# Attention heads: the key and query loads of a head as two transfers of 64 rows each, in place of one with an outermost count of two

## The chip, the cores and the metric

The kernel runs on one core of one Trainium2 chip. The metric is the device time of one execution in microseconds (us), smaller is better. Matrix products run on TensorE (PE in the profile; PEld is its weight load), element-wise work on VectorE (DVE), ScalarE (ACT) and GpSimd (POOL). Transfers between DRAM and the on-chip buffer are issued from the queues of SyncE (SP) and of GpSimd, and 16 DMA engines carry them out.

## The reference

One layer of a decoder trunk: a norm, a combined input projection, four token mixers (two attentions, a recurrent branch, attention into a memory), gates, and a gated MLP. The change touches the loads of the two attentions with 16 heads of 64 columns over 1024 tokens:

```python
        fq = _rms(_heads(proj("fox_q"), FOX_HEADS), fox_q_norm_g[l]).astype(f32)
        fk = _rms(_heads(proj("fox_k"), FOX_HEADS), fox_k_norm_g[l]).astype(f32)
...
        # _fox_attention, per block of 128 queries
        logits = jnp.einsum('bhqd,bhkd->bhqk', qi, k) * scale + (fi[..., :, None] - cum_f[..., None, :])
        logits = jnp.where(k_pos[None, :] <= q_pos[:, None], logits, -jnp.inf)
        p = jax.nn.softmax(logits, axis=-1)
        return jnp.einsum('bhqk,bhkd->bhqd', p, v)
...
        # _stick_breaking_attention, per block of 128 queries
        z = jnp.einsum('bhqd,bhkd->bhqk', qi, k) * scale
        log_1m_beta = jnp.where(causal, jax.nn.log_sigmoid(-z), 0.0)
        excl = lax.cumsum(log_1m_beta, axis=3, reverse=True) - log_1m_beta
        weights = jnp.where(causal, jnp.exp(jax.nn.log_sigmoid(z) + excl), 0.0)
        return jnp.einsum('bhqk,bhkd->bhqd', weights, v)
```

## The kernel before

Values are kept as a rounded part and a remainder (two numbers per value), and products are made from two or three matmuls. The kernel works in stages: projections that need a norm of their own (from 0 to about 450 us), the recurrent branch (to about 750 us), the attention stage (about 750 to 1895 us), then the branch projections and the MLP.

In the attention stage three lists of groups run one after the other: the memory attention (`Mem`, 750 to 870 us), the 16 fox heads and the 16 stick-breaking heads (`Head`). Each head has four groups of two query blocks. A group makes scores (`score`: matmuls `S<-kx,qq` on L182, two per piece of up to 512 keys), a softmax or a scan on ACT, DVE and POOL, transposes of the weights (`turn`, `T` on L848, evacuated on L613 and L614) and the product with the values (`value`, `PV` on L182). Between these, matmuls of the remaining projections and gates (`mm<-hTh,wh` and the like, also L182) are put in as filler, one by one, by `fill`. The order of all PE work of the stage is written out when the program is made, by a planner in `build` that keeps a model of the engines' times (`clock`, `spend`); on the chip it is fixed, and PE takes its instructions in that order.

The loads of a head are all issued from the POOL queue: `load_q` loads the queries `qq` (L736, 1 MB: 64 rows of 8 KB, twice, into the two halves of the 128 partitions) and for fox the row of forget sums `fb`, copied to 128 partitions (L733); `load_k` loads `kx` (L750, 512 KB: the rounded keys into partitions 0 to 63, the remainders into 64 to 127); `load_v` loads `vx` (L756, 512 KB, 128 partitions as the outermost count). In `load_q` and `load_k` the source has an outermost count of two, and under it 64 rows. `qq`, `kx` and `vx` have two buffers each. A head's loads are issued when the head two before it has finished its last scores (`qq`, `kx`) or its last values (`vx`).

POOL also computes. For a fox head it makes `fd` from `fb` (`offsets`, L744) ahead of the head's scores; this is issued when the head before it is halfway through its scores. For a stick-breaking head it makes the two triangular masks of every query block (`affine_select`, L829), for which the scan on DVE (L831) waits. POOL takes its loads and its computing in one order, so a `fd` that waits for `fb` holds back the loads behind it.

Of the kernel before, what the change touches and what calls it, by code (L numbers as in the profile page):

```python
# [7 lines left out]
F32 = mybir.dt.float32  # L8
# [8 lines left out]
S = 1024  # L17
# [4 lines left out]
HD = 64  # L22
# [40 lines left out]
def build(tc, a, out):  # L63
    nc = tc.nc
# [8 lines left out]
    fk_d = dp.tile([2, D, S], F32, name="fk_d")  # L73
    sq_d = dp.tile([D, 2, S], F32, name="sq_d").rearrange("d t s -> t d s")
    sk_d = dp.tile([2, D, S], F32, name="sk_d")
# [402 lines left out]
    with ExitStack() as s1:  # L478
# [140 lines left out]
        class Mem:  # L619
# [8 lines left out]
            def load_q(self):  # L628
                h, g = self.h, self.g
                r0 = h * 256  # L630
                mq = aq.tile([P, 2, 2, 512], F32R, tag="qq", name="mq")
                for i in range(2):
                    nc.gpsimd.dma_start(mq[:, i].bitcast(F32), mq_d[i, r0:r0 + 256, g * 256:g * 256 + 512].rearrange(
                        "(k p) n -> p k n", p=P))
                Mem.loaded[h, "q", g // 2] = mq

            def load_k(self):
                h = self.h
                r0 = h * 256
                mk = aq.tile([P, 2, 2, NM], F32R, tag="kx", name="mk")  # L640
                for i in range(2):
                    nc.gpsimd.dma_start(mk[:, i].bitcast(F32), mk_d[i, r0:r0 + 256, :].rearrange("(k p) n -> p k n", p=P))
                Mem.loaded[h, "k"] = mk
# [73 lines left out]
        class Head:  # L717
# [9 lines left out]
            def load_q(self):  # L727
                fox, h = self.fox, self.h
                qd = fq_d if fox else sq_d
                fb = fd = None  # L730
                if fox:
                    fb = ap.tile([P, S], F32, tag="fg", name="fb", bufs=4)
                    nc.gpsimd.dma_start(fb, fb_d[h:h + 1, :].broadcast_to([P, S]))  # L733
                    fd = ap.tile([P, S], F32, tag="fg", name="fd", bufs=4)
                qq = aq.tile([P, 2, S], F32R, tag="qq", name="qq")
                nc.gpsimd.dma_start(qq.rearrange("p t n -> p (t n)").bitcast(F32), qd[:, h * HD:(h + 1) * HD, :].rearrange(  # L736
                    "t p n -> p (t n)").unsqueeze(0).broadcast_to([2, HD, 2 * S]))
                Head.loaded[fox, h, "q"] = (qq, (fb, fd))

            def offsets(self):  # L740
# [6 lines left out]
            def load_k(self):  # L747
                fox, h = self.fox, self.h
                kx = aq.tile([P, S], F32R, tag="kx", name="kx")
                nc.gpsimd.dma_start(kx.bitcast(F32), (fk_d if fox else sk_d)[:, h * HD:(h + 1) * HD, :])  # L750
                Head.loaded[fox, h, "k"] = kx

            def load_v(self):
# [130 lines left out]
        fox = range(16, 16 + 4 * NH)  # L884
# [28 lines left out]
        while vi < len(vq):  # L913
            now = clock["pe"] - (HOPF if vq[vi][0] in fox else HOP)
            if vi < ti:
                n, jp = vq[vi]
# [11 lines left out]
            if ti < len(vq) and ti - vi < PHB and slots["T"][-BANKS[1]] <= now:  # L928
                n, jp = vq[ti]
# [4 lines left out]
            if si < len(sq) and slots["S"][-BANKS[0]] <= now:  # L934
                n, f = sq[si]
# [113 lines left out]
    for p in range(NFF // 2):  # L1049
# [4 lines left out]
        for f in range(2):  # L1054
            n = 2 * p + f
# [58 lines left out]
```

## Time and profile before

| | us |
|---|---|
| median of 3 runs | 3077.54 (3076.27 to 3084.1) |
| the profiled execution | 3077.55, with a span of 3075.7 from its first to its last instruction |
| PE busy | 2930.7 (95% of the span) |
| DVE busy | 1726.9 (56%) |
| ACT busy | 1271.9 (41%) |
| POOL busy | 288.1 (9%) |

Busy time is that of one engine; the span is not their sum, since they run side by side. What lies around the span is 1.85 us. A row of idle time tells how long an engine stood still ahead of a group of instructions, and what ended that. The granted clock is that of TensorE, 1.00 for 2.4 GHz and 0.50 for 1.2 GHz. Shares of DMA are means over the 16 engines.

### The profile page before, as it was taken

To read this page: it belongs to the slowest core of one execution; us is meant where nothing else is said; L and a number is where in the kernel's file an instruction comes from. 1 tells how busy PE (TensorE), PEld (TensorE's weight loads), DVE (VectorE), ACT (ScalarE), POOL (GpSimd) and SP (SyncE) were. 2 spreads that over 40 slices of the span, in tenths; PEclk is the share of its full clock that TensorE was granted. 3 is DMA by queue.
4 is the path that set the end of the run, shared out by engine and by line. 5 is a ranking of instruction groups with operands and counts; after the bars stand their busy time and mean duration, and the time that the engine had idled before them with its cause. 6 is when DMAs were issued, how large, how long until landed. Compare 5 with 4: busy or idle time off the path is not lost.

```text
span 3075.7 us, 38719 instructions
## 1 busy us (share of the span) xinstructions
PE 2930.7 (95%) x14800; PEld 2474.8 (80%) x14800; DVE 1726.9 (56%) x3261; ACT 1271.9 (41%) x2264; POOL 288.1 (9%) x438
## 2 busy tenths in 40 slices
PE   8999999999978889888999999999999999999999
PEld 6888888887867778777888888888898888888887
DVE  7664235566546666657898994243454444444443
ACT  5333223676435556556666663222333222222211
POOL 0000000001201111112443330000000000000000
PEclk9999999999989999999999999999999999999999
DMA  6445543123654444444443435434332111111111
GB/s 209 136 144 185 164 146 118 59 75 128 224 152 145 136 155 140 123 123 133 119 135 117 137 114 182 135 128 141 132 109 83 55 55 42 55 42 41 62 35 55
DMA packets 267242, 358.98 MB, mean 117 GB/s; under 512 B 71137, under 2 KB 198145, under 8 KB 262961
## 3 DMA queue, kind: packets, MB, share of 16 engines
q1 hardware_dynamic: 189744, 267.49, 27.0%
q0 software_dynamic: 77312, 89.02, 9.5%
q8 instruction: 117, 1.92, 0.2%
q14 instruction: 69, 0.56, 0.1%
HBM read 255.50 MB, written 100.73 MB: 116 GB/s over the span
## 4 chain that ended last, share of the span: by engine, by line
PE 71%; DMA 18%; DVE 3%; ACT 3%; issue 3%; POOL 2%; SPq 0%; POOLq 0%; DVEq 0%; ACTq 0%
PE mm L189 19%; PE up L189 15%; PE mmb L189 13%; DMA fb<-fb_d 9%; PE mm L182 8%; PE dn L189 8%; DMA kx<-sk_d 5%; PE PV L182 3%; PE S L182 2%; DMA kx<-fk_d 2%; PE T L848 1%; DMA wr<-in_w_in_dram 1%; DMA yr<-y_d 1%; PE T L303 1%; POOL gm L829 1%
## 5 line engine op out<-in xcount | busy, mean ns | idle before, releaser
L182 PE MATMUL mm<-hTh,wh 128*128 128x512 f32 x768 | 310.0, 404 | 1.9 <-DVE fs L589 1.9
L182 PE MATMUL mm<-hTl,wh 128*128 128x512 f32 x768 | 309.8, 403 | 0.0
L182 PE MATMUL mm<-hTh,wl 128*128 128x512 f32 x768 | 309.2, 403 | 0.0
L182 PE MATMUL S<-kx,qq 128*128 128x512 f32 (+2 forms) x768 | 200.6, 363 | 99.4 <-DMA kx<-fk_d 56.2
L189 PE MATMUL up<-h2h,wh 128*128 128x512 f32 x704 | 274.2, 390 | 0.0
L189 PE MATMUL up<-h2h,wl 128*128 128x512 f32 x704 | 274.2, 389 | 0.0
L189 PE MATMUL up<-h2l,wh 128*128 128x512 f32 x704 | 274.0, 389 | 0.0
L132 DVE TENSOR_TENSOR wl<-wr,wh 128x1024 fp32r<-128x1024 f32 (+1 forms) x216 | 207.0, 986 | 111.2 <-ACT wh L131 110.9
L189 PE MATMUL mm<-wh,hTh 128*128 128x512 f32 x640 | 255.6, 399 | 2.3 <-ACT hTh L131 2.3
L189 PE MATMUL mm<-wh,hTl 128*128 128x512 f32 x640 | 251.6, 393 | 0.2 <-DVE hTl L132 0.2
L189 PE MATMUL mm<-wl,hTh 128*128 128x512 f32 x640 | 250.7, 392 | 0.0
L131 ACT CAST wh<-wr 128x1024 fp32r<-128x1024 f32 (+1 forms) x216 | 176.6, 863 | 178.4 <-PE mmb L189 75.2
L182 PEld LDWEIGHTS S<-kx,qq 128*128 128x128 f32 x768 | 134.6, 196 | 125.4 <-issue 97.6
L614 DVE TENSOR_TENSOR pl<-T,ph 128x512 fp32r<-128x512 f32 (+1 forms) x336 | 203.2, 632 | 56.4 <-ACT ph L613 55.4
L613 ACT CAST ph<-T 128x512 fp32r<-128x512 f32 (+1 forms) x336 | 172.7, 553 | 125.8 <-PE T L848 113.6
L189 PE MATMUL mmb<-yh,wh 128*128 128x512 f32 x512 | 198.3, 390 | 4.4 <-ACT yh L131 4.4
L189 PE MATMUL mmb<-yl,wh 128*128 128x512 f32 x512 | 199.3, 390 | 0.6 <-DVE yl L132 0.6
L189 PE MATMUL mmb<-yh,wl 128*128 128x512 f32 x512 | 198.7, 389 | 0.0
L831 DVE TENSOR_TENSOR_SCAN gm<-gm 128x128 f32<-128x128 f32 (+7 forms) x128 | 174.4, 1375 | 23.3 <-POOL gm L829 23.0
L1078 DVE TENSOR_TENSOR x<-x,dn 128x512 f32<-128x512 f32 x176 | 120.0, 687 | 101.6 <-PE dn L189 101.6
L182 PEld LDWEIGHTS mm<-hTh,wh 128*128 128x128 f32 x768 | 148.4, 193 | 28.4 <-DVE fs L589 2.4
L182 PEld LDWEIGHTS mm<-hTh,wl 128*128 128x128 f32 x768 | 148.4, 193 | 25.5
(270 smaller groups left out, 6365.8 us busy)
## 6 DMA issues: line engine op xcount, KB each, us to landing
wr<-in_w_in_dram SPq DMA_DIRECT2D x104, 512.0 KB, 5.0
wr<-in_w_up_dram SPq DMA_DIRECT2D x44, 512.0 KB, 3.5
qq<-fq_d POOLq DMA_DIRECT2D x16, 1024.0 KB, 27.7
gate_d<-gs SPq DMA_DIRECT2D x64, 256.0 KB, 7.1
qq<-sq_d POOLq DMA_DIRECT2D x16, 1024.0 KB, 26.4
wr<-in_w_branch_dram SPq DMA_DIRECT2D x32, 512.0 KB, 4.7
yr<-y_d SPq DMA_DIRECT2D x32, 512.0 KB, 4.3
gt<-gate_d SPq DMA_DIRECT2D x32, 512.0 KB, 4.0
```

The lines of the kernel that those rows point to most:

```text
L131: nc.scalar.copy(hi, src)
L132: nc.vector.tensor_tensor(lo, src, hi, op=ALU.subtract)
L182: pe(nc.tensor.matmul(*args, **kw))
L189: ins = nc.tensor.matmul(ps, l, r, start=(i == 0 and j == 0), stop=(i == n - 1 and j == 2))
L303: nc.tensor.transpose(ptv[:, f, :], qn[:, f * P:(f + 1) * P], ident)
L613: nc.scalar.copy(ph[:, :n], t[:, :n])
L614: nc.vector.tensor_tensor(pl[:, :n], t[:, :n], ph[:, :n], op=ALU.subtract)
L829: nc.gpsimd.affine_select(out=d[:, w - P:w], in_=d[:, w - P:w], compare_op=ALU.is_gt, fill=v, base=0, pattern=[[-1, P]], channel_multiplier=1)
L831: nc.vector.tensor_tensor_scan(gm[:, 0:w][:, ::-1], gm[:, 0:w][:, ::-1], gm[:, 0:w][:, ::-1], 1.0, op0=ALU.mult, op1=ALU.min)
L848: pe(nc.tensor.transpose(t[:, n * P:(n + 1) * P], self.prs[qi][:, j * P:(j + 1) * P], ident))
L1078: nc.vector.tensor_tensor(x2[t][:, sl], x2[t][:, sl], ps, op=ALU.add)
```

## The change

In `load_q` and in `load_k` the one transfer becomes a loop over the two halves of the partitions. Each turn issues a transfer whose outermost count is 64 rows. The bytes, their places, the buffers and the queue stay as they are; `vx`, `fb` and the loads of `Mem` are not touched.

```diff
                 qq = aq.tile([P, 2, S], F32R, tag="qq", name="qq")
-                nc.gpsimd.dma_start(qq.rearrange("p t n -> p (t n)").bitcast(F32), qd[:, h * HD:(h + 1) * HD, :].rearrange(
-                    "t p n -> p (t n)").unsqueeze(0).broadcast_to([2, HD, 2 * S]))
+                for i in range(2):
+                    nc.gpsimd.dma_start(qq[i * HD:(i + 1) * HD].rearrange("p t n -> p (t n)").bitcast(F32),
+                                        qd[:, h * HD:(h + 1) * HD, :].rearrange("t p n -> p (t n)"))
                 Head.loaded[fox, h, "q"] = (qq, (fb, fd))
...
                 kx = aq.tile([P, S], F32R, tag="kx", name="kx")
-                nc.gpsimd.dma_start(kx.bitcast(F32), (fk_d if fox else sk_d)[:, h * HD:(h + 1) * HD, :])
+                for i in range(2):
+                    nc.gpsimd.dma_start(kx[i * HD:(i + 1) * HD].bitcast(F32),
+                                        (fk_d if fox else sk_d)[i, h * HD:(h + 1) * HD, :])
                 Head.loaded[fox, h, "k"] = kx
```

## Rows read from the trace of the kernel before

**Rows 1.** The page: granted clock in 40 slices, and the chain's shares by line.
```profile
PEclk9999999999989999999999999999999999999999
PE mm L189 19%; PE up L189 15%; PE mmb L189 13%; DMA fb<-fb_d 9%; PE mm L182 8%; PE dn L189 8%; DMA kx<-sk_d 5%; PE PV L182 3%; PE S L182 2%; DMA kx<-fk_d 2%; PE T L848 1%; DMA wr<-in_w_in_dram 1%; DMA yr<-y_d 1%; PE T L303 1%; POOL gm L829 1%
```

**Rows 2.** Busy time by engine: the fox heads, then the stick-breaking heads.
```profile
core 0: us, PE busy (x) PEld busy (x) DVE busy (x) ACT busy (x) POOL busy (x), PEclk, DMA share, GB/s
870.00:1375.00 505.00, 425.87 (x2397) 370.36 (x2397) 305.48 (x1014) 259.80 (x524) 72.07 (x72) 0.92 0.45 135
1375.00:1860.00 485.00, 452.42 (x2676) 394.74 (x2675) 417.37 (x554) 315.54 (x691) 176.96 (x304) 0.98 0.41 124
```

**Rows 3.** Groups of PE, 870 to 1375 us: busy, mean ns | idle before, ended by.
```profile
L182 PE MATMUL S<-kx,qq 128*128 128x512 f32 (+2 forms) x362 | 97.6, 370 | 78.8 <-DMA kx<-fk_d 56.2 <-issue 17.3 <-DVE mx L799 4.1
```

**Rows 4.** The same view, 1375 to 1860 us.
```profile
L182 PE MATMUL S<-kx,qq 128*128 128x512 f32 (+2 forms) x406 | 103.0, 356 | 20.6 <-DMA kx<-sk_d 19.2 <-ACT ph L613 0.6 <-DVE mx L799 0.5
...
L848 PE MATMUL T<-ident,pr 128*128 128x128 f32 x627 | 87.3, 274 | 6.8 <-DVE pr L834 6.7
L182 PE MATMUL PV<-pl,vx 128*128 128x256 f32 (+1 forms) x352 | 86.4, 285 | 5.2 <-DVE pl L614 5.1
```

**Rows 5.** POOL in order of time, one fox head: start, us, instruction [idle before].
```profile
1210.03 2.40 POOL L744 TENSOR_TENSOR fd<-fb,mask 128x1024 f32<-128x1024 f32 x1 [24.80 <-DMA fb<-fb_d]
1212.39 0.59 POOL L756 DMA_DIRECT2D vx<-fv_d  x1
1212.97 0.81 POOL L736 DMA_DIRECT2D qq<-fq_d  x1
1213.76 0.59 POOL L733 DMA_DIRECT2D fb<-fb_d  x1
1214.32 0.83 POOL L750 DMA_DIRECT2D kx<-fk_d  x1
1243.45 2.33 POOL L744 TENSOR_TENSOR fd<-fb,mask 128x1024 f32<-128x1024 f32 x1 [28.30 <-DMA fb<-fb_d]
```

**Rows 6.** DMA issues, whole run: count, KB of each, median us to landing.
```profile
qq<-fq_d POOLq DMA_DIRECT2D x16, 1024.0 KB, 27.7
...
fb<-fb_d POOLq DMA_DIRECT2D x16, 512.0 KB, 27.8
kx<-fk_d POOLq DMA_DIRECT2D x16, 512.0 KB, 28.8
vx<-fv_d POOLq DMA_DIRECT2D x16, 512.0 KB, 4.3
...
kx<-sk_d POOLq DMA_DIRECT2D x16, 512.0 KB, 25.0
```

**Rows 7.** The tile view of `fb`: its landing over 16 loads.
```profile
DMA to landing us min/median/max: 5.6/27.8/32.1
```

**Rows 8.** DMA from 1201 to 1204 us, POOL's queue: packets, MB, share of 16.
```profile
q0 software_dynamic: 20, 0.16, 12.9%
```

**Rows 9.** Busy time (columns as Rows 2) of four stretches in which few loads are awaited.
```profile
1060.00:1140.00 80.00, 79.45 (x471) 69.74 (x470) 59.96 (x193) 47.28 (x97) 10.20 (x10) 1.00 0.50 159
1206.00:1240.00 34.00, 34.00 (x203) 29.98 (x203) 24.38 (x78) 22.64 (x46) 5.12 (x5) 1.00 0.50 142
1480.00:1515.00 35.00, 33.70 (x199) 29.39 (x198) 31.85 (x39) 25.20 (x57) 15.13 (x24) 1.00 0.48 140
1670.00:1740.00 70.00, 68.70 (x413) 60.16 (x413) 63.01 (x78) 47.80 (x107) 25.11 (x46) 1.00 0.39 123
```

**Rows 10.** The same columns: the ten fox stretches at the lower clock, two and sum.
```profile
875.30:892.30 17.00, 4.99 (x15) 4.35 (x16) 2.87 (x18) 1.80 (x6) 0.00 (x0) 0.50 0.26 99
...
1144.90:1155.20 10.30, 4.87 (x16) 4.23 (x17) 1.63 (x6) 1.63 (x4) 5.05 (x5) 0.50 0.38 100
...
sum 78.40, PE 42.51 PEld 37.38 DVE 13.61 ACT 15.93 POOL 29.96; mean PE 4.25 PEld 3.74 DVE 1.36 ACT 1.59 POOL 3.00
```

**Rows 11.** PE in order of time around the start of one fox head.
```profile
1239.91 0.39 PE L182 MATMUL mm<-hTh,wh 128*128 128x512 f32 x1
1240.14 0.39 PE L182 MATMUL mm<-hTl,wh 128*128 128x512 f32 x1
1246.21 0.77 PE L182 MATMUL S<-kx,qq 128*128 128x256 f32 x2 [5.68 <-DMA kx<-fk_d]
1246.78 0.63 PE L182 MATMUL mm<-hTh,wl 128*128 128x512 f32 x1
1247.20 0.63 PE L182 MATMUL mm<-hTh,wh 128*128 128x512 f32 x1
```

**Rows 12.** POOL's groups, 750 to 1860 us, and DVE's scan, 1375 to 1860 us.
```profile
L750 POOL DMA_DIRECT2D kx<-sk_d x16 | 12.8, 800 | 0.6 <-issue 0.4
L756 POOL DMA_DIRECT2D vx<-sv_d x16 | 9.2, 575 | 62.7 <-PE T L848 61.6 <-issue 1.2
L831 DVE TENSOR_TENSOR_SCAN gm<-gm 128x128 f32<-128x128 f32 (+7 forms) x128 | 174.4, 1375 | 23.3 <-POOL gm L829 23.0
```

## The prediction

> **What bounds the kernel now.** I read the page first. Its chain of waits goes mostly through PE, but 16% of the span are loads of `fb` and `kx`, and the clock dips only in the attention slices [rows 1]. So I took the busy time by engine of the two kinds of heads. In the 505 us of the fox heads PE is busy 425.9 us, DVE 305, ACT 260, at a mean clock of 0.92: no engine is full. In the 485 us of the stick-breaking heads PE is busy 452.4 us and DVE 417 [rows 2]. The groups of PE then tell where the idle 79 us of the fox heads lie: all of it stands before the scores `S<-kx,qq`, 78.8 us, and 73.5 of that ended with the keys' load, or at the "issue" of the first head, where nothing but its loads was late [rows 3]. For the stick-breaking heads it is 20.6 us before the scores, 19.2 of them for `kx`; another 12 us stand before transposes and value products and wait for DVE [rows 4].
>
> Why a load takes so long is seen on the DMA side. `qq` (1 MB) lands after 27.7 us and `kx` (512 KB) after 28.8, while `vx`, as large as `kx` and issued from the same queue, lands after 4.3 [rows 6]. The difference that the code shows is the outermost count: 128 for `vx`, two for the others. From 1201 to 1204 us POOL's queue moves only the 8 KB rows of `qq`: 20 packets in 12.9% of 16 engines, so 2.06 engines at work, 0.129 x 16 x 3 / 20 = 0.31 us a row [rows 8]. Two engines need 64 x 0.31 = 19.8 us for the 128 rows. `fb` has 128 rows and can land in 5.6 us, but its median is 27.8 [rows 7]: it is issued 0.8 us behind `qq`, and I read that as what stands behind `qq` landing only after it.
>
> That closes a loop on POOL. `fd` waits 25 to 28 us for `fb`; the loads of the next head but one stand behind it and go out only then, `fb` again behind `qq` [rows 5]. One turn is the landing plus some 5 us of POOL, 33.4 us between the two `fd` shown, and 505/16 = 31.6 us on the mean. PE has less work than that in a head, so it stands before the next scores: 5.68 us in the head shown [rows 11].
>
> **The change part by part.** *The landing.* With 64 rows as the outermost count I expect a half to spread over the engines as `vx` does. The trace has no 64-row load from this queue. Bounds: two engines (nothing gained), or 16. By the 0.31 us per 8 KB of [rows 8], 16 engines move 423 GB/s. The 2.62 MB of a fox head (`qq`, `fb`, `kx`, `vx`) take 6.2 us alone and some 12 us where the queues share the engines equally. I take 5 to 12 us for each load, the side of `vx`. The exact count hardly matters: on only four engines the four halves (1.57 MB at 106 GB/s) take 14.8 us, and they have a whole head of time.
>
> The Trainium skill, "DMA: Bandwidth & Descriptors", section "Why a DMA increments its semaphore by 16 and not by 1", says that the slowest dimension's size decides how many of the 16 engines carry a transfer, which gives two before and 16 after. By it the halves take the 6.2 us of the 16-engine bound and the sum below stays as it is; the two engines of [rows 8] agree, and no row before can show the 16.
>
> *The fox heads.* The loop on POOL becomes landing + 2.4 (`fd`) + about 3.4 (issues), 11 to 18 us, below a head's PE work. So the 78.8 us before the scores go [rows 3]. The clock gains too. The ten stretches at 0.50 (1.2 GHz) last 78.4 us, follow the waits and hold 42.5 us of PE work [rows 10]. A matmul of 512 columns comes every 0.42 us there and every 0.23 at full clock [rows 11]. The work then shrinks by 42.5 x (1 - 0.23/0.42) = 19.2 us, as long as PE has no more such waits. 505 - 78.8 - 19.2 = 407 us. Cross-check: in the stretch from 1060 to 1140 us, at clock 1.00, 471 records take 79.45 busy us of 80, 0.1687 each [rows 9]; 2397 records [rows 2] give 404, and 407 with that stretch's 0.7% idle. What is late next is PE itself: DVE's 305 us are 75% of 407, as in that stretch (60 of 80), where PE hardly stood. Gain 98 us.
>
> *The stick-breaking heads.* No `fd` holds POOL here, so the waits are short. The waits before the scores go; those for DVE stay. By the two stretches at full clock, 0.1693 and 0.1663 us a record at 96.3% and 98.1% busy [rows 9], 2676 records [rows 2] take 453/0.963 = 470 or 445/0.981 = 454 us. I take 461, nearer to the longer stretch. DVE would be busy 417/461 = 90%, just as in that stretch (63 of 70), so it is close behind PE. Gain 24 us.
>
> *The issues.* 64 loads become 128. A load with the count of two costs POOL 0.80 to 0.83 us, one of 128 rows 0.58 [rows 5, 12]. A half is bounded by half of that, 0.29, and by 0.83; I take 0.55, near the 128-row load. A head then has 4 x 0.55 = 2.2 in place of 1.6 us, so +0.6, and from -0.4 to +1.7 by the bounds. In the fox heads this is covered by POOL's idle time. In the stick-breaking heads masks are queued behind it, and the scan waits for masks 23.0 us now [rows 12]. 16 heads x 0.6 = 10 us at most (-7 to +27 by the bounds), of which I count 3, since DVE is not last there. Without that cover it is the whole 10.
>
> *Sum*, against the profiled execution's 3077.55, which is the median of the runs to 0.01: -98 - 24 + 3 = -119, so 2958 us. Everything before 870 and after 1860 us stays.
>
> **The rivals.** *New waits take up a part.* PE's order is written out beforehand, and PE's waits gave DVE and ACT time to catch up. For it: the waits for DVE in the stick-breaking heads [rows 4], at 86% DVE. Against it: 80 us of fox heads ran without a wait [rows 9]. If the fox heads come to 430 us, for which DVE and PSUM waits of 5% must appear, and the others to 475, it gives -75 - 10, so 2993.
>
> *The landing isn't shortened* (the change doesn't do what it says): two engines still carry a half, or the halves run one behind the other. For it: no row shows a 64-row load. Against it: `vx`. The two issues ahead of `fb` then stand in the POOL loop; 16 x 0.3 us gives 3082.
>
> The skill's same page, in "Rules for kernel authors", advises against two transfers to disjoint halves of the partitions: both would use the same engines and serialize, so one transfer over 128 is as good. By that rule this rival holds. The rows speak against it here, since the transfer that is split uses two engines [rows 8].
>
> *Slower.* The issue itself is dear: 0.83 us for each half, with a landing that stays near 28 us. Each fox turn grows by 2 x 0.83 - 0.81 = 0.85 us, 14 us in all. The masks of the stick-breaking heads wait 16 x 1.7 = 27 us more, of which half reaches DVE's scan: 3077.5 + 14 + 14 = 3105. It decides only where `fb` lands so late that the POOL loop exceeds a head's PE work of 407/16 = 25.4 us, so after about 20 us; below that, dear issues alone cost at most 27 us of a gain of 122.
>
> **How the numbers follow.** 80% for the forecast, 12% for the new waits, 5% for no shorter landing (3082), 3% for slower. The likeliest time is 2958. The lower end is PE's work at full clock alone: 404 + 445 us in place of 990 gives 2937, which no stretch of the second kind reaches, so 2940. The upper end takes in the new waits and the dear issues, 3005; what is left out is 8% and the tails. A measurement of this kernel tells about 0.3% (9 us) from no change. Faster 0.92, same 0.05, slower 0.03.
>
> **What would show it.** In the profile after: `qq`, `kx` and `fb` land in 5 to 12 us; POOL's share of 16 engines comes in short bursts; `fd` hardly waits for `fb`, and POOL's waits become those for free buffers (PE's scores). The idle time before `S<-kx,qq` falls from 78.8 and 20.6 us to a few, the clock stays at 1.00 from 870 to 1860 us, and PE's 2397 and 2676 records take about 407 and 461 us. DVE is near 75% and 90% there. The issues of a half show 0.3 to 0.8 us. The prediction is wrong if the landing stays above 20 us, if transposes, value products or scores wait for DVE or ACT by more than 30 us in all, or if the masks' wait before the scan grows by more than 10 us.

## The result and the profile after

| | us | ratio to before (95% interval) |
|---|---|---|
| before, median | 3077.8 | |
| after, median of 4 (2981.4 to 2987.2) | 2983.2 | 0.969 (0.967 to 0.971) |
| the profiled execution after | 2983.88, span 2982.2 | |

94.6 us less, where 119 were forecast (2958, range 2940 to 3005). The direction and the range held, and so did the mechanism in the fox heads; the gain forecast for the stick-breaking heads did not come. A fifth of the whole is missing, and the experiments below look for it. The times here and below are medians without single runs in a slow state (one of 10.3 ms with the fox heads alone, one of 5.9 ms with quarters).

DMA issues of the profile after, with count, KB of each and median us to landing; they answer to [rows 6].

```profile
qq<-fq_d POOLq DMA_DIRECT2D x32, 512.0 KB, 7.1
...
fb<-fb_d POOLq DMA_DIRECT2D x16, 512.0 KB, 7.4
kx<-fk_d POOLq DMA_DIRECT2D x32, 256.0 KB, 9.6
...
kx<-sk_d POOLq DMA_DIRECT2D x32, 256.0 KB, 6.9
```

What took 25 to 29 us now takes 7 to 10. `fb`, which the change does not touch, came down with the others, from 27.8 to 7.4: it had stood behind `qq`, as the experiment on single loads below shows.

How many engines carry a half can be read where a half of `qq` is alone on POOL's queue, from 1589 to 1590 us (columns of [rows 8]):

```profile
q0 software_dynamic: 40, 0.33, 114.6%
```

40 rows of 8 KB start in 1 us, against 20 in 3 us in [rows 8], six times as fast, and their time fills all 16 engines. (A row counts whole in the stretch in which it starts, hence more than 100%.)

Waits of POOL in the fox heads after (total us, times, longest), and busy time in the columns of [rows 2], with the clock:

```profile
POOL qq L737 <- PE S L182: 106.1, 10, 18.1
POOL vx L759 <- PE PV L182: 85.7, 14, 11.1
POOL fd L745 <- DMA fb<-fb_d: 60.6, 11, 6.7
```

```profile
866.00:1280.00 414.00, 406.64 (x2392) 354.60 (x2392) 320.08 (x1006) 254.23 (x516) 80.45 (x103) 1.00 0.60 166
1283.00:1768.00 485.00, 455.47 (x2677) 398.12 (x2676) 412.65 (x560) 317.77 (x695) 181.79 (x334) 0.98 0.44 123
```

The POOL loop is open: its longest wait for `fb` is 6.7 us where single waits of 25 to 28 stood [rows 5], and POOL now waits for buffers that PE still reads. The fox heads run with PE 98% busy and the clock at 1.00. For the stick-breaking heads a stretch of the same length holds as many records as before (2677 and 2676, [rows 2]) at the same clock: nothing was gained there.

Where the 93.5 us of the two spans lie is read from the first scores of the stick-breaking heads (the one row of each trace below, before, then after) and from the tile view of `kx`, which has its first and last start:

```profile
1407.08 0.77 PE L182 MATMUL S<-kx,qq 128*128 128x256 f32 x2 [6.74 <-DMA kx<-sk_d]
```

```profile
L182 PE MATMUL S<-kx,qq x768: 274/387/629, 887.3 to 1844.3; 128*128 128x512 f32 x96, 128*128 128x384 f32 x64, 128*128 128x256 f32 x32
```

```profile
1309.57 0.39 PE L182 MATMUL S<-kx,qq 128*128 128x256 f32 x2
```

```profile
L182 PE MATMUL S<-kx,qq x768: 274/364/668, 869.0 to 1752.4; 128*128 128x512 f32 x96, 128*128 128x384 f32 x64, 128*128 128x256 f32 x32
```

Up to the first stick-breaking score 1407.1 - 1309.6 = 97.5 us are gained, 6.7 of them the wait ahead of it, so 91 by the fox heads. From there to the last score it is 437.2 before and 442.8 after: 5.6 us are lost again, so that the stick-breaking heads gain 1 us in all. The rest of the span, 1231.4 and 1229.8 us, gives 1.6.

The groups of PE in the stick-breaking heads after (1283 to 1768 us), answering to [rows 4]:

```profile
L182 PE MATMUL S<-kx,qq 128*128 128x512 f32 (+2 forms) x406 | 103.0, 357 | 1.4 <-ACT pr L812 1.1 <-DVE mx L802 0.4
L851 PE MATMUL T<-ident,pr 128*128 128x128 f32 x627 | 91.7, 280 | 14.1 <-DVE pr L837 14.1
...
L182 PE MATMUL PV<-pl,vx 128*128 128x256 f32 x350 | 87.6, 290 | 14.0 <-DVE pl L614 14.0
```

The 20.6 us before the scores are 1.4 now, as forecast. But the waits for DVE, forecast to stay at 12 us, are 28. The clock, too, was forecast at 1.00 and is 0.98. Three stretches at the lower level, 0.50, make it up (columns of [rows 2]; the last of them, and the sum of the three):

```profile
1604.20:1611.00 6.80, 5.97 (x23) 5.59 (x24) 5.69 (x11) 2.49 (x6) 0.54 (x2) 0.50 0.43 121
sum 17.10, PE 15.36 PEld 14.59 DVE 10.76 ACT 8.53 POOL 1.62; mean PE 5.12 PEld 4.86 DVE 3.59 ACT 2.84 POOL 0.54
```

They begin at 1433.5, 1495.0 and 1604.2 us, each during or just after one of PE's three longest waits for `pl`, of 2.8, 2.2 and 4.0 us. One place shows how DVE comes to be late. It is the end of the tenth stick-breaking head, DVE in order of time, first before, then after:

```profile
1691.03 1.31 DVE L834 TENSOR_TENSOR pr<-pr,gm 128x1023 f32<-128x1023 f32 x1
1692.26 1.08 DVE L831 TENSOR_TENSOR_SCAN gm<-gm 128x128 f32<-128x128 f32 x2
...
1696.95 1.88 DVE L614 TENSOR_TENSOR pl<-T,ph 128x512 fp32r<-128x512 f32 x3
```

```profile
1594.12 1.32 DVE L837 TENSOR_TENSOR pr<-pr,gm 128x1023 f32<-128x1023 f32 x1
1599.20 0.69 DVE L614 TENSOR_TENSOR pl<-T,ph 128x512 fp32r<-128x512 f32 x1 [3.76 <-ACT ph L613]
1599.81 1.00 DVE L834 TENSOR_TENSOR_SCAN gm<-gm 128x128 f32<-128x128 f32 x2
```

After the product `pr` with 1023 columns, DVE before went on with the scans of the next head's first blocks, which were ready, and evacuated later. After, an evacuation `pl` stands ahead of these scans; it needs a transpose of the `pr` just made and a cast on ACT, so DVE stands 3.76 us with ready work behind it. PE's wait of 4.0 us, ended by a `pl`, follows at 1601 us. DVE's order is another one, though no line of the change touches DVE.

### The profile page after: what moved, and what is told of

It is laid out like the page before. It is cut to its first block, busy times and chain, and to the rows that moved or that the text cites. A ratio compares the mean times of both kernels' runs of the same rounds, so it can differ in the third digit from the quotient of the medians.

```text
span 2982.2 us, 38824 instructions
## 1 busy us (share of the span) xinstructions
PE 2913.9 (98%) x14800; PEld 2461.8 (83%) x14800; DVE 1737.7 (58%) x3261; ACT 1270.0 (43%) x2264; POOL 301.9 (10%) x502
## 3 DMA queue, kind: packets, MB, share of 16 engines
q1 hardware_dynamic: 189744, 267.49, 27.8%
## 5 line engine op out<-in xcount | busy, mean ns | idle before, releaser
L851 PE MATMUL T<-ident,pr 128*128 128x128 f32 x1152 | 162.4, 277 | 14.1 <-DVE pr L837 14.1
L182 PE MATMUL PV<-pl,vx 128*128 128x256 f32 (+1 forms) x640 | 159.8, 288 | 14.2 <-DVE pl L614 14.1
```

The costliest lines, as they stand in the source:

```text
L182: pe(nc.tensor.matmul(*args, **kw))
L851: pe(nc.tensor.transpose(t[:, n * P:(n + 1) * P], self.prs[qi][:, j * P:(j + 1) * P], ident))
```

## The experiments

Listing the instructions of each built program gives, engine by engine, where the orders differ:

```
                      PE     ACT    DVE    POOL
instructions before   14802  2088   3263   443
instructions after    14802  2088   3263   507
places that differ    0      0      149    362
```

DVE's differences begin where the stick-breaking heads do; the 64 more on POOL are the loads, and they shift the places of what follows. The order is laid out when the program is built; it came out otherwise with other loads on POOL.

**DVE's order tied to the one before, with the split loads, and the other way round.** Both kernels add the same lines behind the attention loop; only the string of the order differs (`made` collects the scans, products, evacuations, sums and remainders as they are emitted). In the traces PE and ACT have one and the same order in all of these kernels.

```diff
+        order = (
...
+        )
+        at = {"s": 0, "m": 0, "p": 170, "y": 31, "w": 163}
+        last = None
+        for c in order:
+            ins = made[c][at[c]]
+            at[c] += 1
+            if last is not None:
+                tc.add_manual_dep(ins.ins, last.ins.name, NOSYNC, reason="order")
+            last = ins
```

> The kernel with the split loads, but with VectorE's order in the stick-breaking heads tied to the one that the kernel before has there: the scans of a head's first query blocks ahead of the evacuations pl of the head before it. PE's and ScalarE's orders are the same in all these kernels. Theory A (order): the 24 us that were forecast for the stick-breaking heads are lost because the program that was built from the split loads gives VectorE another order, in which pl, which waits for a transpose and a cast, stands ahead of scans that are ready. Then VectorE's idle time before pl falls from 41 to about 20 us, PE's idle time before transposes and value products from 28 to about 12, and the time from 2983 to 2955 to 2968 us. Theory B (limit): VectorE and PE bound these heads in any order, and a wait that is removed comes back elsewhere: 2978 to 2988 us.

> The kernel before (loads with an outermost count of two), with VectorE's order in the stick-breaking heads tied to the one that the kernel with the split loads has there. Theory A (order): the idle time before pl grows by some 20 us and PE's before transposes and value products by some 10 to 15, beside the waits for the keys that stay; a part falls into those waits, so 3077 + 5 to 20, that is 3082 to 3097 us. Theory B (limit): 3074 to 3081 us, no change.

Measured: 2970.5 us (ratio 0.965, 0.963 to 0.967) with the split loads and the old order, and 3090.5 us (1.0043, 1.0029 to 1.0057) with the old loads and the new order. Run side by side on one chip:

> The changed kernel itself, beside the next run on the same chip: 2980 to 2987 us.

> The split loads with VectorE's old order, beside the run before on the same chip. Theory A (order): 10 to 16 us less than that. Theory B (chip to chip): less than 5 us.

2981.7 (0.969, 0.967 to 0.970) and 2968.8 us (0.9645, 0.963 to 0.966): the order alone is worth 12.9 us with the split loads and 14 with the old ones. The same added lines gain in the one kernel and cost in the other, so it is the order and not the lines. The order is a cause; both times with the old one lie just above the range that was expected of it (2955 to 2968), so it is not the only one. PE's and DVE's groups with the split loads and the old order (1283 to 1768 us):

```profile
L853 PE MATMUL T<-ident,pr 128*128 128x128 f32 x627 | 88.1, 275 | 9.6 <-DVE pr L839 9.5
L184 PE MATMUL PV<-pl,vx 128*128 128x256 f32 x354 | 87.4, 287 | 10.3 <-DVE pl L616 10.2
```

```profile
L616 DVE TENSOR_TENSOR pl<-T,ph 128x512 fp32r<-128x512 f32 (+1 forms) x176 | 104.2, 625 | 15.5 <-ACT ph L615 15.4
```

DVE's idle time before `pl` is 15.5 us; in the changed kernel it was 41.5:

```profile
L614 DVE TENSOR_TENSOR pl<-T,ph 128x512 fp32r<-128x512 f32 (+1 forms) x175 | 104.1, 627 | 41.5 <-ACT ph L613 41.3
```

PE's waits for DVE fell from 28 to 20 us, not to 12. Their longest is 1.9 us now, and the clock is at 1.00 from 1283 to 1768 us. The first score of the stick-breaking heads, and the tile view of `kx` with the last:

```profile
1310.33 0.39 PE L184 MATMUL S<-kx,qq 128*128 128x256 f32 x2
```

```profile
L184 PE MATMUL S<-kx,qq x768: 274/343/504, 870.1 to 1737.9; 128*128 128x512 f32 x96, 128*128 128x384 f32 x64, 128*128 128x256 f32 x32
```

From the one to the other it is 427.6 us, against 442.8 with the new order. Of these 15 us, 8 are PE's shorter waits. The clock's part is estimated as the prediction does it for the fox heads: the 15.4 us of PE work at 0.50 would shrink by 15.4 x (1 - 0.23/0.42), so by 7. With the old order the stick-breaking heads gain 16 us over the kernel before (437.2 and the 6.7 of wait ahead of them, less 427.6), where 21 were forecast; the fox heads gain as much as with the new one.

**The two kinds of heads apart.** The loops stand under `if fox:` (or `if not fox:`), with the old loads under `else:`; for `qq` the same.

```diff
+                if fox:
                     for i in range(2):
                         nc.gpsimd.dma_start(kx[i * HD:(i + 1) * HD].bitcast(F32),
                                             (fk_d if fox else sk_d)[i, h * HD:(h + 1) * HD, :])
+                else:
+                    nc.gpsimd.dma_start(kx.bitcast(F32), (fk_d if fox else sk_d)[:, h * HD:(h + 1) * HD, :])
```

> The split loads for the fox heads alone; the stick-breaking heads load as before, and VectorE keeps the order of the kernel before there. Both theories: the fox heads give their 92 to 98 us, and the stick-breaking heads keep the 20 us of waits for the keys. Theory A (order): the kept waits cost about what the new order costs, so 2976 to 2986 us with 20 us idle before the scores and 12 before transposes and value products. Theory B (limit): the same time, 2978 to 2988, but the idle time before transposes and value products grows towards 28 us, since VectorE has less time to catch up after faster fox heads.

> The split loads for the stick-breaking heads alone; the fox heads load as before. VectorE has the new order there. Theory A (order): the waits for the keys (20 us) go, those before transposes and value products rise from 12 to about 28, clock about as before: 3070 to 3083 us. Theory B (limit): also no gain, 3074 to 3081. If instead the gain is 15 us or more (3062 or less), the loss in the changed kernel comes from the faster fox heads ahead of these heads and not from the stick-breaking heads' own order.

Measured: 2982.9 us (0.969, 0.966 to 0.971) for fox alone, the time of the whole change, and 3076.4 (0.9994, 0.998 to 1.0006) for the stick-breaking heads alone, no change. The groups of PE in the stick-breaking heads: first with fox alone (1283 to 1768 us), then with the stick-breaking heads alone (1375 to 1860 us):

```profile
L182 PE MATMUL S<-kx,qq 128*128 128x512 f32 (+2 forms) x406 | 103.2, 356 | 19.2 <-DMA kx<-sk_d 18.8 <-DVE mx L809 0.4
...
L858 PE MATMUL T<-ident,pr 128*128 128x128 f32 x627 | 87.2, 274 | 6.4 <-DVE pr L844 6.3
L182 PE MATMUL PV<-pl,vx 128*128 128x256 f32 x350 | 85.8, 285 | 4.4 <-DVE pl L614 4.3
```

```profile
L182 PE MATMUL S<-kx,qq 128*128 128x512 f32 (+2 forms) x408 | 102.9, 355 | 5.2 <-DMA kx<-fk_d 3.7 <-ACT pr L819 1.1 <-DVE mx L809 0.4
L858 PE MATMUL T<-ident,pr 128*128 128x128 f32 x627 | 91.6, 279 | 15.1 <-DVE pr L844 15.1
...
L182 PE MATMUL PV<-pl,vx 128*128 128x256 f32 x348 | 86.8, 289 | 14.1 <-DVE pl L614 14.0
```

The one pays for the keys and 11 us for DVE, the other 29 us for DVE and little for the keys. Faster fox heads ahead do not raise the waits for DVE, as theory B had it; the new order that the stick-breaking heads' own split loads bring does.

**What is left with the old order.** Some 5 of the 21 us are still missing. Two kernels take load off DVE, each with the split loads and the old order. The first shortens `pl` to 128 columns, which PE's products then read for all of them (those lines are left out here):

```diff
-            made["p"].append(nc.vector.tensor_tensor(pl[:, :n], t[:, :n], ph[:, :n], op=ALU.subtract))
+            d = P if short else n
+            made["p"].append(nc.vector.tensor_tensor(pl[:, :d], t[:, :d], ph[:, :d], op=ALU.subtract))
```

> Split loads with VectorE's old order, and in the stick-breaking heads the remainder pl of the weights is made for the first 128 columns alone and used for all (the remainders of the other columns are left out). Every wait and every instruction stays; VectorE has about 70 us less to do (174 evacuations of 0.2 in place of 0.62 us), and one evacuation's delay is 0.4 us shorter. Theory A (VectorE's load is what is left): of the 20 us that PE still waits before transposes and value products at most 6 stay, and the time falls from 2970 to 2952 to 2960 us. Theory B (ScalarE, POOL's masks or the written-out order): the waits stay above 14 us and the time is 2964 to 2972.

Measured: 2948.8 us (0.958, 0.956 to 0.959), 21.7 less than with the whole `pl`. The evacuations took 0.31 us on the mean, not 0.2, so DVE lost 55 us and not 70. This run alone leaves open whether the load or the earlier end of each evacuation did it. The second leaves out the remainders `wl` of part of the filler's weights, work that stands beside that chain:

```diff
-                split(wr[:, ks, :], wh[:, kd, :], wl[:, kd, :])
+                if low:
+                    split(wr[:, ks, :], wh[:, kd, :], wl[:, kd, :])
+                else:
+                    nc.scalar.copy(wh[:, kd, :], wr[:, ks, :])
```

> Split loads with VectorE's old order; the remainders wl of the filler weights that are made beside the stick-breaking heads (nine pairs of gates) are left out, and the rounded weights are used in their place. PE's instructions and order stay. VectorE loses 36 instructions of 0.70 us, 25 us, none of which stands in the chain from transposes to value products. Theory A (VectorE's load is what is left): the shorter pl took 55 us from VectorE and gave 22, so 25 us give 8 to 12: 2957 to 2964 us. Theory B (the shorter pl helped because each evacuation came sooner, not because VectorE had less to do): 2967 to 2973 us.

Measured: 2958.8 us (0.962, 0.960 to 0.963), 10 to 11.7 less than the two runs with all remainders, as theory A had it. DVE had waited only 2.6 us in all ahead of these `wl`, so what went with them is work and not waiting. So PE does gain when DVE has less to do. The same 400 us of the four kernels, in the columns of [rows 2]: the change, the old order, without `wl`, with the short `pl`. All four start the stick-breaking heads within 2 us of 1309, so the count of PE's records tells how far each gets.

```profile
1310.00:1710.00 400.00, 372.43 (x2180) 325.81 (x2179) 342.25 (x430) 262.45 (x581) 163.01 (x300) 0.98 0.45 125
```

```profile
1310.00:1710.00 400.00, 380.18 (x2268) 331.39 (x2267) 362.12 (x450) 271.60 (x600) 175.94 (x311) 1.00 0.48 132
```

```profile
1310.00:1710.00 400.00, 385.43 (x2316) 338.42 (x2315) 351.21 (x424) 276.87 (x614) 170.05 (x313) 1.00 0.48 132
```

```profile
1310.00:1710.00 400.00, 394.64 (x2380) 347.15 (x2379) 330.92 (x469) 284.12 (x629) 177.97 (x319) 1.00 0.48 133
```

With the new order DVE is 86% busy and PE gets through 2180 records; with the old one 91% and 2268. As DVE's load falls to 88 and 83%, PE rises from 95 to 96 and 99%. From the first to the last score it is 420.1 us without `wl` and 409.9 with the short `pl`, in place of 427.6.

**Which load it was.** Only one of the two loops stays, the other load is as before; with the queries split alone:

```diff
-                for i in range(2):
-                    nc.gpsimd.dma_start(kx[i * HD:(i + 1) * HD].bitcast(F32),
-                                        (fk_d if fox else sk_d)[i, h * HD:(h + 1) * HD, :])
+                nc.gpsimd.dma_start(kx.bitcast(F32), (fk_d if fox else sk_d)[:, h * HD:(h + 1) * HD, :])
```

> Only the query load is split; the key load keeps its outermost count of two. Theory A (what is issued behind a load on two engines lands after it): the key load's two engines need 64 rows of 4 KB, about half of the 0.31 us of an 8 KB row, 10 us, so kx lands in 11 to 16 us and fb in 6 to 12. The POOL loop becomes 12 to 17 us, below the 25 us of PE work in a head: the fox heads give their whole 92 to 98 us, and the time is 2968 to 2990 us with whatever order VectorE has in the stick-breaking heads. Theory B (each load is late by its own count of two alone, and both matter): the keys stay the last to arrive, half of the gain: 3020 to 3050 us.

> Only the key load is split; the query load keeps its outermost count of two and needs at least 64 x 0.31 = 19.8 us on two engines. Theory A: fb and kx are issued behind it and land with it, after 22 to 28 us, so the POOL loop stays at 27 to 33 us and the fox heads give 0 to 25 us: 3050 to 3078 us. Theory B: fb and kx land in 5 to 12 us, since their own transfers are on 16 engines; POOL is free early, only qq is late by its 20 to 25 us, which a head's PE work just covers, and the time is 2985 to 3020 us.

Measured: 2983.3 us (0.970, 0.968 to 0.971) with the queries split, the time of the whole change, and 3075.9 (0.999, 0.998 to 1.000) with the keys split, nothing. DMA issues, first with the queries split, then with the keys split:

```profile
qq<-fq_d POOLq DMA_DIRECT2D x32, 512.0 KB, 7.4
fb<-fb_d POOLq DMA_DIRECT2D x16, 512.0 KB, 7.1
kx<-fk_d POOLq DMA_DIRECT2D x16, 512.0 KB, 19.6
```

```profile
qq<-fq_d POOLq DMA_DIRECT2D x16, 1024.0 KB, 28.3
fb<-fb_d POOLq DMA_DIRECT2D x16, 512.0 KB, 28.6
kx<-fk_d POOLq DMA_DIRECT2D x32, 256.0 KB, 29.5
```

Theory A holds. With the keys split, their halves still land after 29.5 us, behind `qq`, and `fb` after 28.6; here what stands behind the slow transfer on the queue is as late as that transfer. With the queries split, `kx` on its own takes 19.6 us, later than the 11 to 16 expected, and costs nothing: no wait of PE for `kx` is left in either kind of head, since a head has 25 us for it. That the time equals that of the whole change is in part chance: DVE has a third order there, and PE's waits for DVE in the stick-breaking heads are 27 us (28 with the whole change).

**The price of issues.** Each half is cut again, into 32 rows (`qq` in the same way), with the old order of DVE.

```diff
-                for i in range(2):
-                    nc.gpsimd.dma_start(kx[i * HD:(i + 1) * HD].bitcast(F32),
-                                        (fk_d if fox else sk_d)[i, h * HD:(h + 1) * HD, :])
+                for i in range(4):
+                    r0 = h * HD + (i % 2) * 32
+                    nc.gpsimd.dma_start(kx[i * 32:(i + 1) * 32].bitcast(F32),
+                                        (fk_d if fox else sk_d)[i // 2, r0:r0 + 32, :])
```

> Split loads with VectorE's old order, and each half cut again: four transfers of 32 rows for qq and four for kx. It measures the price of more issues on POOL: a head has 8 issues in place of 4. Theory A (POOL's issues are covered): 32-row issues take 0.45 to 0.52 us, POOL gains 1.6 to 2.0 us a head, 26 to 32 us in the stick-breaking heads, of which the scans' waits for masks take 0 to 8: 2968 to 2980 us. Theory B (masks behind the issues hold VectorE): 25 us or more on top, 2990 us and above. The landing stays at 5 to 11 us if 32 rows still spread over all 16 engines; on fewer it doubles.

Measured: 2986.0 us (0.970, 0.969 to 0.972), 15.5 more than with halves. POOL's issues and DVE's scan (1290 to 1780 us):

```profile
L740 POOL DMA_DIRECT2D qq<-sq_d x64 | 31.5, 495 | 49.9 <-PE S L184 47.7 <-issue 2.1
L756 POOL DMA_DIRECT2D kx<-sk_d x64 | 30.9, 490 | 2.7 <-issue 2.6
```

```profile
L838 DVE TENSOR_TENSOR_SCAN gm<-gm 128x128 f32<-128x128 f32 (+7 forms) x128 | 175.0, 1380 | 15.8 <-POOL gm L836 15.3
```

An issue of 32 rows costs 0.49 us, one of 64 rows 0.52: nearly all of it does not depend on the rows. 62.4 us of issues in place of 33.0 raise the scans' wait for masks from 9.2 us (halves, old order) to 15.3, so about a fifth of the added time reaches DVE; from the first to the last score it is 433.9 us in place of 427.6. More is lost in the fox heads, 12 us from their first score to the first of the others (440.3 to 452.0), where PE's waits of the scores for DVE grow from 7.3 to 12.6 us; the cause stays open. Theory A named the size of the issues rightly and the total too low.

## Why the prediction was right, and where it was not

- **What bounds the kernel: right.** The wait for the loads held the fox heads, by way of POOL: with `qq` alone split the loop is open, with `kx` alone split it stays shut.
- **The landing: right,** 7 to 10 us of the 5 to 12 expected. The 16 engines that no row before could show are seen in the row from 1589 to 1590 us above. (The 6.2 us that the prediction names for the halves are its figure for all four loads of a head, 2.62 MB; the sum does not use them.)
- **The fox heads: right, 7 us too high.** 98 forecast, 91 measured. The clock term held (1.00). What is missing is in PE's waits for DVE before the scores, forecast as nothing:

```profile
PE S L182 <- DVE mx L802: 6.9, 7, 2.6
```

- **The stick-breaking heads: wrong.** 21 us of gain forecast (24, less 3 for the issues), 1 measured. The step that failed is the rate from two stretches of the trace before: it took for granted that DVE's program stays as it is, that waits for DVE stay at 12 us, and that the clock is at 1.00. None of this held. The order of DVE changed with the build, 13 us, longer waits for `pl` and the lower clock behind them together. And DVE at about 90% is not "close behind" but already holds PE in part: with the old order PE still waits 20 us for it, and some 5 us of the forecast stay away. (The other 7 of the 12 us between 2970 and 2958 are those of the fox heads.) That DVE's load holds PE is shown by the kernels without `wl` and with the short `pl`, 10 to 22 us faster; that it makes up just these 5 us is not. Both stretches follow a wait for keys, in which DVE could catch up; that this made them look better is argued, not shown.
- **Its own signs.** The prediction called itself wrong if PE waited for DVE or ACT by more than 30 us in all. From 866 to 1768 us it is 36.5: 14.1 before transposes, 14.1 before value products, 8.3 before scores. This sign pointed at the step that failed, though the time lies in the range.
- **The issues: the size right, the 3 us not seen.** A half costs 0.52 us (0.55 taken), so a head pays 2.08 in place of 1.6 us. But the scan's wait for masks, 23.0 us before [rows 12], did not grow: it is 7.6 us after, and 9.2 with the old order.
- **The rivals.** New waits were named, with 2993 us and 12%. What happened lies between the forecast and it: waits for DVE at high load, as this rival had it, and a mechanism that was not named, the build's order. The advice of the Trainium skill ("DMA: Bandwidth & Descriptors", "Rules for kernel authors") against two transfers to disjoint halves does not hold here, where the one transfer ran on two engines: 3077.8 became 2983.2 us.

The best kernel of the study is the change with DVE's old order, 2969 to 2970 us.

## What to carry to other kernels

Look at the outermost count of every transfer that lands late, and at what stands behind it on its queue: splitting the one load of 1 MB freed those behind it and a computing engine. When a wait is removed, price the next engine at the load that it will then have: here DVE, at about 90%, left PE waiting 20 us. And compare the instruction order of all engines after any change of loads: here an order that nobody wrote took back 13 us.

## What was not expected of the hardware

A fixed DVE instruction became longer without any change to it. The scaling of the fox weights on DVE by its shapes, before, then after (mean ns of one):

```profile
L824 DVE TENSOR_SCALAR pr<-pr,sm 128x512 f32<-128x512 f32 x15 | 7.3, 486 | 0.5
L824 DVE TENSOR_SCALAR pr<-pr,sm 128x384 f32<-128x384 f32 x15 | 6.3, 417 | 0.1
```

```profile
L827 DVE TENSOR_SCALAR pr<-pr,sm 128x512 f32<-128x512 f32 x15 | 13.7, 913 | 0.5
L827 DVE TENSOR_SCALAR pr<-pr,sm 128x384 f32<-128x384 f32 x15 | 12.4, 826 | 0.1
```

One of them, and `fd` on POOL at the same time:

```profile
1021.66 2.19 DVE L827 TENSOR_SCALAR pr<-pr,sm 128x512 f32<-128x512 f32 x1
1023.77 0.68 DVE L614 TENSOR_TENSOR pl<-T,ph 128x512 fp32r<-128x512 f32 x1
```

```profile
1021.17 2.40 POOL L745 TENSOR_TENSOR fd<-fb,mask 128x1024 f32<-128x1024 f32 x1 [6.46 <-DMA fb<-fb_d]
```

It begins 0.5 us into `fd` and ends 0.3 us after it, 2.19 us for what takes 0.49 on the mean before. Before, `fd` ran while PE waited for the keys, from 1243.45 to 1245.78 us in the head shown [rows 5, 11]. The Trainium skill, "SBUF — State Buffer", section "SBUF: two separate sides", says that VectorE's modes with two ports and GpSimd share a pair of ports that one of them holds for a whole instruction while the other is blocked; these rows agree, though none shows the mode. Over all its shapes the scaling takes DVE some 16 us more in the fox heads. That a part of PE's 7 us there comes from it is possible, but no run here shows it.
